# Second layer of a two-layer streaming encoder step: decays per batch, diagonal inverses, inner outputs in a shared bank

## Chip, core and metric

The kernel runs on one core of a Trainium2 chip. The metric is the time of one execution on the device, in microseconds (us). Before the change it is 1435.36 us, the median of three runs (1433.28 to 1436.85).

The engines are called PE (TensorE, matrix products), DVE (VectorE), ACT (ScalarE), POOL (GpSimd) and SP (SyncE, which here only issues transfers). Each works through its own queue in order. PE reads SBUF and writes PSUM; DVE and ACT read and write both; POOL is used on SBUF alone.

## The reference

The step has two layers over 1024 prompt frames and 64 sample frames of width 1024. The first has a gated convolution and band attention. The second, which the change touches, is a gated delta rule with 8 heads of width 128, in chunks of 64 frames (16 of the prompt, one of the sample, each group with its own start state):

```python
def gdn_chunk(S, q, k, v, g, beta):
    gc = jnp.cumsum(g, axis=1)
    decay = jnp.exp(jnp.where(incl, gct[..., :, None] - gct[..., None, :], -jnp.inf))
    kk = jnp.einsum('blhd,bmhd->bhlm', k, k)
    a = jnp.where(strict, bt[..., :, None] * kk * decay, 0.0)
    tmat = a + jnp.eye(L)
    rhs = concatenate([v * beta, k * (beta * exp(gc))])
    sol = triangular_solve(tmat, rhs, lower=True, unit_diagonal=True)
    u = sol[..., :HD_C] - einsum(sol[..., HD_C:], S)
    qk = einsum(q, k) * decay
    o = einsum(q * exp(gc), S) + einsum(qk, u)
    S_new = exp(g_last) * S + einsum(k * exp(g_last - gc), u)
```

Here `incl` is the lower triangle with its diagonal and `strict` the one without. Since `g` is negative, `gc` falls along a chunk, so the difference in `decay` is never positive where it is used.

## The kernel before

Activations lie with channels on the 128 partitions. A weight tile is 128 x 128 for each of eight k-tiles; every projection is made of three products (`hi` by `hi`, `hi` by `lo`, `lo` by `hi`) into a PSUM tile `pjt`, over three groups of 384, 384 and 320 frames. These `pjt<-...` products are most of PE's work in both layers.

The order of work on PE is written by the program itself: generators are registered with the class `Order`, and each `yield` names a time in ns after which the generator may go on, or the name of something that must be done. `Order.run` walks them by rank against a running estimate of PE's time. On the other engines the order comes from a scheduler of the tile framework, which also sets the waits.

In the second layer (`odd`) the heads are handled as four pairs, and the 17 chunks of a pair in three batches of 6, 6 and 5, so there are twelve batches. While `main` projects q, k and v of the next pair and, at the end, the gates z, each batch goes through these generators:

- `gates` (once): the cumulated decays `gc` and their exponentials, for all pairs.
- `decays` (once): for every pair and batch, the differences of `gc` between frames. DVE puts `gc` on a diagonal (L912), PE spreads it with a product of a block matrix (`tr<-dbuf,cst`), DVE subtracts (L916), POOL adds one of two masks with -1e30 outside a triangle (L919), ACT takes `Exp` (L920), and ACT's queue writes the strict and the transposed form to `Dd` in DRAM (L921).
- `prepare` (`prep`): loads the two decay tiles `Dst` and `DT`, transposes keys and queries on PE (`tr<-cst,kq`), takes squares on ACT (`junk`), makes key products (`tr<-kq`), and from them `An` and `KQD` (L984, L985). `Af`, the four diagonal 16 x 16 blocks of each head's matrix, is written to `Sd` in DRAM.
- `substitute` (`sub`): reads it back as `AL`, with one block in each of 48 partitions, does forward substitution in 14 steps of two POOL instructions (L1009, L1010), and writes the inverses to a second `Sd`.
- `join` (`inv`): loads the inverses as `Xf`, and POOL multiplies them with two masks into X, 32 wide with blocks on the diagonal (L1038). DVE transposes X into XT (L1039); PE products `tr<-XT,Cb`, `tr<-M,X` and `tr<-XT,An` put the larger inverse together.
- `solve` (`wy`): transposes and products that give the two right-hand sides.
- `scan`: chunk after chunk. PE makes `ks<-S,kq` (keys and queries on the state, two quarters of a PSUM bank), DVE `us` (L1158) and ACT `qs` (L1160) read it; PE makes `su<-us,kd`, and DVE two new states `S` (L1172). The inner outputs of the chunk before (`tr<-us,KQD`) are made in a `tr` bank just ahead of `ks`, and DVE adds `qs` to them (`o`, L1127).
- `finish`: normalizes four chunks of outputs and writes them to `od`.

The PSUM pool `pg` has two banks `tr`, which all of these share, two `su`, and one `ks`; the framework lets two engines read one PSUM tile only one behind the other (ACT's `qs` waits for DVE's `us`). A batch's `prep` waits for the `prep` before it, for `wy` two before and for `scan` three before; `sub` waits for the `sub` before it.

Of the kernel before, what the change touches and what calls it, by code (L numbers as in the profile page):

```python
# [7 lines left out]
F32 = mybir.dt.float32  # L8
# [31 lines left out]
C_M1, C_M2 = 448, 512  # L40
# [16 lines left out]
def constants():  # L57
# [10 lines left out]
    c[:, C_M1:C_M1 + 64] = np.where(j[None, :] < i[:, None], 0.0, NEG)  # L68
    c[:, C_M2:C_M2 + 64] = np.where(j[None, :] >= i[:, None], 0.0, NEG)
# [38 lines left out]
class Net:  # L108
# [124 lines left out]
    def run(self):  # L233
# [4 lines left out]
        with tc.tile_pool(name="pj", bufs=2, space=PSUM) as self.pj:  # L238
# [15 lines left out]
            self.Dd = [dram.tile([P, NCH, 64], F32, name=f"Dd{i}") for i in range(8)]  # L254
            self.Sd = [[dram.tile([m, P, 16], F32, name=f"Sd{a}{b}") for b, (c0, m) in enumerate(BATCHES)] for a in range(2)]
# [504 lines left out]
    def odd(self):  # L760
        nc, tc, I, O = self.nc, self.tc, self.I, self.O
        act, dve, pool, par, cst = self.act, self.dve, self.pool, self.par, self.cst
        w_in, mix, order, Dd, od, Sd = I["w_in1"], self.mixd[1], self.order, self.Dd, self.od, self.Sd
# [135 lines left out]
        def decays():  # L899
            gc = G["gc"]  # L900
            buf = G["buf"]

            def part(i, m):
                return buf[:, 384 * i:384 * i + 64 * m].rearrange("p (c j) -> p c j", j=64)

            for p in range(4):
                yield 0
                for c0, m in BATCHES:
                    sh = [P, m, 64]
                    gcb = gc[:, p, c0:c0 + m].unsqueeze(2).broadcast_to(sh)  # L910
                    gx, df = part(0, m), part(1, m)
                    dve.tensor_tensor(gx, gcb, cst[:, C_ID64:C_ID64 + 64].unsqueeze(1).broadcast_to(sh), ALU.mult)  # L912
# [3 lines left out]
                    dve.tensor_tensor(df, ps[:, :64 * m].rearrange("p (c j) -> p c j", j=64), gcb, ALU.subtract)  # L916
                    for q, (cm, op) in enumerate(((C_M1, ALU.subtract), (C_M2, ALU.add))):
                        dx = part(2 + q, m)
                        pool.tensor_tensor(dx, cst[:, cm:cm + 64].unsqueeze(1).broadcast_to(sh), df, op)  # L919
# [3 lines left out]
                order.done.add(f"dec{p}")  # L923
# [423 lines left out]
```

## Time and profile before

| what | value |
|---|---|
| median of the runs shown | 1435.36 us |
| profiled execution | 1453.08 us, its span 1451.3 us |
| mean granted PE clock of the profiled execution | 0.973 |
| busy share of the span: PE, DVE, ACT, POOL | 95%, 58%, 47%, 20% |
| second layer from the first decay to the last scan | about 690 to 1305 us |
| gates and output projection after it | to 1451 us |

The page gives busy time per engine and groups of instructions. A group names the line of the kernel (a helper's line for all products: L119 and L124), the engine, and output and input by tile names: `tr<-XT,Cb` is a product into a `tr` bank. Behind the bar stand the busy time, the mean of one instruction, and the idle time before it with its releaser. The views by windows give the same for stretches of time, with the granted clock of PE. Spans on POOL are rough.

### The profile page before, as it was taken

To read this page: it belongs to the slowest core of one execution; us is meant where nothing else is said; L and a number is where in the kernel's file an instruction comes from. 1 tells how busy PE (TensorE), PEld (TensorE's weight loads), DVE (VectorE), ACT (ScalarE), POOL (GpSimd) and SP (SyncE) were. 2 spreads that over 40 slices of the span, in tenths; PEclk is the share of its full clock that TensorE was granted. 3 is DMA by queue.
4 is the path that set the end of the run, shared out by engine and by line. 5 is a ranking of instruction groups with operands and counts; after the bars stand their busy time and mean duration, and the time that the engine had idled before them with its cause. 6 is when DMAs were issued, how large, how long until landed. Compare 5 with 4: busy or idle time off the path is not lost. (4 is left out here: it accounts for less than half of the span.)

```text
span 1451.3 us, 27914 instructions
## 1 busy us (share of the span) xinstructions
PE 1378.2 (95%) x10600; PEld 1238.7 (85%) x10600; DVE 839.1 (58%) x2220; ACT 676.9 (47%) x1776; POOL 289.8 (20%) x590
## 2 busy tenths in 40 slices
PE   8999999999999999899887999999999989999996
PEld 6989998998999899788776778778877877889995
DVE  7575257237436754786884668555765665433554
ACT  7643344144234456675554454435443534333752
POOL 3001000000100014420353325120423151300122
PEclk9999999999999999999998999999999999999998
DMA  8402111210210264540431112122321132336753
GB/s 270 132 23 82 57 52 52 79 53 27 89 61 30 81 234 141 188 145 31 115 96 52 29 40 71 27 42 49 71 34 42 37 100 59 98 104 205 244 199 117
DMA packets 113831, 132.71 MB, mean 91 GB/s; under 512 B 35280, under 2 KB 80792, under 8 KB 113696
## 3 DMA queue, kind: packets, MB, share of 16 engines
q1 hardware_dynamic: 82448, 104.32, 24.7%
q10 hardware_dynamic: 31248, 26.60, 5.7%
q8 instruction: 83, 1.36, 0.4%
q14 instruction: 52, 0.43, 0.1%
HBM read 99.71 MB, written 34.31 MB: 92 GB/s over the span
## 5 line engine op out<-in xcount | busy, mean ns | idle before, releaser
L119 PE MATMUL pjt<-hhi,wlo 128*128 128x384 f32 (+1 forms) x1768 | 618.7, 350 | 1.9 <-DVE wlo L165 1.9
L119 PE MATMUL pjt<-hhi,whi 128*128 128x384 f32 (+1 forms) x1768 | 584.8, 331 | 7.8 <-ACT whi L164 4.9
L119 PE MATMUL pjt<-hlo,whi 128*128 128x384 f32 (+1 forms) x1768 | 577.3, 330 | 1.1 <-DVE hlo L418 1.1
L119 PEld LDWEIGHTS pjt<-hhi,wlo 128*128 128x128 f32 x1768 | 338.0, 191 | 26.2 <-issue 12.4
L119 PEld LDWEIGHTS pjt<-hhi,whi 128*128 128x128 f32 x1768 | 338.5, 191 | 14.6 <-ACT whi L164 6.1
L119 PEld LDWEIGHTS pjt<-hlo,whi 128*128 128x128 f32 x1768 | 336.7, 191 | 2.0 <-DVE hlo L418 2.0
L165 DVE TENSOR_TENSOR wlo<-wf,whi 128x512 fp32r<-128x512 f32 x222 | 151.6, 707 | 165.8 <-ACT whi L164 162.1
L164 ACT CAST whi<-wf 128x512 fp32r<-128x512 f32 x222 | 130.4, 619 | 164.9 <-PE pjt L119 118.9
L639 ACT ACTIVATE pr<-pr,mx 128x640 f32<-128x640 f32 (+5 forms) x72 | 50.9, 707 | 89.4 <-DVE mx L638 88.9
L797 DVE SCALAR_TENSOR_TENSOR kq<-pjt,par,kq 128x384 f32<-128x384 f32 (+2 forms) x144 | 71.6, 497 | 3.4
L375 POOL TENSOR_TENSOR sqa<-sqa,sq 128x384 f32<-128x384 f32 (+1 forms) x36 | 39.3, 1091 | 142.0 <-ACT sq L372 141.9
L600 POOL MEMSET bias<- 64x64 f32 x8 | 1.5, 183 | 320.7 <-DMA bias<-Gd 295.6
L636 DVE CUSTOM_DVE_ANT_0 pr<-sc,bias 128x640 f32<-128x640 f32 (+5 forms) x72 | 47.9, 666 | 26.7 <-PE sc L119 25.9
L1172 DVE SCALAR_TENSOR_TENSOR S<-S,egl,su 128x128 f32<-128x128 f32 x128 | 40.2, 343 | 38.2 <-PE su L119 37.7
L1009 POOL TENSOR_TENSOR px<-AL 48x14 f32<-48x14 f32 (+6 forms) x168 | 46.5, 277 | 44.6 <-DMA AL<-Sd 33.2
L962 ACT ACTIVATE junk<-tr 128x128 f32<-128x128 f32 x136 | 37.7, 277 | 30.1 <-PE tr L124 24.5
L1010 POOL TENSOR_TENSOR AL<-AL,px 48x14 f32<-48x14 f32 (+6 forms) x168 | 48.1, 286 | 11.8
L1131 ACT ACTIVATE junk<-o 128x128 f32<-128x128 f32 x68 | 21.0, 309 | 57.4 <-DVE o L1127 52.4
L124 PE MATMUL pt<-cst,pr 128*128 128x128 f32 (+1 forms) x280 | 43.4, 270 | 4.4 <-DVE pr L641 2.9
L119 PE MATMUL ks<-S,kq 128*64 128x128 f32 x512 | 44.0, 295 | 0.0
L119 PE MATMUL pjt<-mhi,whi 128*128 128x384 f32 x128 | 43.0, 336 | 0.7 <-ACT whi L164 0.7
L119 PE MATMUL pjt<-mhi,wlo 128*128 128x384 f32 x128 | 43.0, 336 | 0.5 <-DVE wlo L165 0.5
(247 smaller groups left out, 2112.0 us busy)
## 6 DMA issues: line engine op xcount, KB each, us to landing
wf<-in_w_in SPq DMA_DIRECT2D x128, 256.0 KB, 3.1
wf<-in_w_out SPq DMA_DIRECT2D x96, 256.0 KB, 3.2
mf<-mixd SPq DMA_DIRECT2D x31, 192.0 KB, 4.2
x<-in_x SPq DMA_DIRECT2D x8, 384.0 KB, 5.5
xg<-in_x SPq DMA_DIRECT2D x2, 1536.0 KB
xd<-xg SPq DMA_DIRECT2D x2, 1536.0 KB
Dd<-dbuf ACTq DMA_DIRECT2D x16, 192.0 KB, 3.1
od<-o ACTq DMA_DIRECT2D x12, 256.0 KB, 2.2
```

The costliest lines, as they stand in the source:

```text
L119: return self.pe.matmul(out, lhsT=lhsT, rhs=rhs, start=start, stop=stop, **k)
L124: return self.pe.transpose(out, in_, self.ident[0:k, 0:k])
L164: self.act.copy(out=hi, in_=x)
L165: (eng or self.dve).tensor_tensor(lo, x, hi.bitcast(F32), ALU.subtract)
L375: pool.tensor_tensor(acc, acc, sq, ALU.add)
L636: dve.tensor_tensor_reduce(out=cut(pr[0:nq, :nk]), in0=sc[0:nq, :nk // nw, :nw], in1=cut(b["bias"][a][0:nq, j0:j0 + nk]), scale=1.0, scala ...
L639: act.activation(pr[0:nq, :nk], pr[0:nq, :nk], AF.Exp, bias=mx[0:nq, 1:2], scale=1.0, accum_out=mx[0:nq, 2:3])
L797: dve.scalar_tensor_tensor(oi, ch(ps[:, i0 + j + 1:i0 + j + 1 + m]), cw[j], oi, ALU.mult, ALU.add)
L962: act.activation(junk, ps[:, i, :], AF.Square, accum_out=ss[:, a, i0 + i:i0 + i + 1])
L1009: pool.tensor_tensor(t, AL[:, j + 1:16, j:j + 1].broadcast_to([lanes, m, w]), x.broadcast_to([lanes, m, w]), ALU.mult)
L1010: pool.tensor_tensor(o, o, t, ALU.add)
L1172: dve.scalar_tensor_tensor(Sn[:, q, :], S[:, q, :], egl[:, q, p, c:c + 1], su[q], ALU.mult, ALU.add)
```

## The change

It has three parts, all in the second layer.

Decays: the generator `decays`, its buffer and the DRAM tiles `Dd` go. Each batch makes its own decay in `prepare`, with a new generator `decay`: the diagonal of `gc` in the tile that becomes `An`, one product on PE, a subtraction by DVE inside the PSUM bank, then on ACT `Abs` and `Exp` with scale -1. So one symmetric tile `E` takes the place of two masked ones. The upper mask is a product on POOL (`KQD` = `E` times a matrix of ones and zeros), the strict lower one a product on DVE over `Af` (16 wide), one instruction more. `prep` waits for `gates` instead of its pair's decays.

Inverses: the second `Sd` is 32 wide, is filled with zeros once by three transfers on ACT's queue, and the inverses are written to its diagonal halves, even blocks left, odd blocks right. So X is loaded as it is, without `Xf` and the two POOL products. `AL` is loaded and the inverses are written in two transfers each, even and odd blocks. In `join` the second `yield` goes from 2250 to 1500.

Outputs: the inner outputs go to the third quarter of the `ks` bank of the next chunk. `outputs` is split: `inner` holds the products and stands where it stood, the DVE addition `o` comes after `us` and `qs`.

```diff
-            for p in range(4):
-                yield 0
-                for c0, m in BATCHES:
...
-                    gx, df = part(0, m), part(1, m)
-                    dve.tensor_tensor(gx, gcb, cst[:, C_ID64:C_ID64 + 64].unsqueeze(1).broadcast_to(sh), ALU.mult)
-                    yield 900
-                    ps = pst("tr")
-                    self.mm(ps[:, :64 * m], cst[:, C_BD:C_BD + P], gx.rearrange("p c j -> p (c j)"))
-                    dve.tensor_tensor(df, ps[:, :64 * m].rearrange("p (c j) -> p c j", j=64), gcb, ALU.subtract)
-                    for q, (cm, op) in enumerate(((C_M1, ALU.subtract), (C_M2, ALU.add))):
-                        dx = part(2 + q, m)
-                        pool.tensor_tensor(dx, cst[:, cm:cm + 64].unsqueeze(1).broadcast_to(sh), df, op)
-                        act.activation(dx, dx, AF.Exp)
-                        nc.scalar.dma_start(Dd[2 * p + q][:, c0:c0 + m, :], dx)
-                    yield 2500
+        def decay(e, gx, p, c0, m):
...
+            dve.tensor_tensor(gx, gcb, cst[:, C_ID64:C_ID64 + 64].unsqueeze(1).broadcast_to(sh), ALU.mult)
+            yield 900
+            ps = pst("tr")[:, :64 * m]
+            self.mm(ps, cst[:, C_BD:C_BD + P], gx.rearrange("p c j -> p (c j)"))
+            ps = ps.rearrange("p (c j) -> p c j", j=64)
+            dve.tensor_tensor(ps, ps, gcb, ALU.subtract)
+            act.activation(e, ps, AF.Abs)
+            act.activation(e, e, AF.Exp, scale=-1.0)
...
-            Dst, DT = bt("Dst", 64), bt("DT", 64)
-            nc.sync.dma_start(Dst, Dd[2 * p][:, c0:c0 + nb, :])
-            nc.sync.dma_start(DT, Dd[2 * p + 1][:, c0:c0 + nb, :])
+            E, An, KQD = bt("E", 64), bt("An", 64, 2), bt("KQD", 64, 3)
+            yield from decay(E, An, p, c0, nb)
...
+            pool.tensor_tensor(KQD, E, cst[:, C_UP:C_UP + 64].unsqueeze(1).broadcast_to([P, nb, 64]), ALU.mult)
...
+            dve.tensor_tensor(Af, Af, cst[:, C_LOW:C_LOW + 16].unsqueeze(1).broadcast_to([P, nb, 16]), ALU.mult)
...
-            nc.sync.dma_start(AL, sa.rearrange("c (b r) j -> (c b) r j", r=16))
+            even = sa.rearrange("c (b t r) j -> t (c b) r j", t=2, r=16)
+            diag = sx.rearrange("c (b t r) (s j) -> t s (c b) r j", t=2, r=16, s=2)
+            half = [slice(0, lanes // 2), slice(lanes // 2, lanes)]
+            for t in range(2):
+                nc.sync.dma_start(AL[half[t]], even[t])
...
-            nc.sync.dma_start(sx.rearrange("c (b r) j -> (c b) r j", r=16), AL)
+            for t in range(2):
+                nc.sync.dma_start(diag[t, t], AL[half[t]])
...
-            Xf = bt("Xf", 16)
-            nc.sync.dma_start(Xf, sx.rearrange("c r j -> r c j"))
+            X, XT = bt("X", 32), bt("XT", 32)
+            nc.sync.dma_start(X, sx.rearrange("c r j -> r c j"))
...
-            for j in range(2):
-                m = cst[:, C_H16 + j:C_H16 + j + 1].unsqueeze(2).broadcast_to([P, nb, 16])
-                pool.tensor_tensor(X[:, :, 16 * j:16 * j + 16], Xf, m, ALU.mult)
...
+                ks = pst("ks") if last or S is not None else None
                 if last:
-                    outputs(*last)
+                    inner(ks[:, 2 * P:3 * P], *last)
                 if S is not None:
-                    ks = pst("ks")
...
                     act.activation(qs, ks[:, P:2 * P], AF.Copy, scale=egc[:, p, c:c + 1])
+                if last:
+                    outputs(ks[:, 2 * P:3 * P], *last)
```

How the edit moves instructions shows at three places. The first is POOL in the substitution of the very first batch. `px` and `AL` are the steps, `dbuf` the decays' mask additions, `rk` and `kt` belong to the next batch's `prepare`. Before:

```order
L971 TENSOR_TENSOR rk<-rk,root 128x6
L1009 TENSOR_TENSOR px<-AL 48x36
L1010 TENSOR_TENSOR AL<-AL,px 48x12x3
L919 TENSOR_TENSOR dbuf<-cst,dbuf 128x384
L1009 TENSOR_TENSOR px<-AL 48x44
L919 TENSOR_TENSOR dbuf<-cst,dbuf 128x384
L975 TENSOR_TENSOR kt<-kt,kap 128x768
L1010 TENSOR_TENSOR AL<-AL,px 48x11x4
```

And after, at the later place where `rk` and `kt` stand now:

```order
L958 TENSOR_SCALAR rk<-ss 128x6
L1004 TENSOR_TENSOR AL<-AL,px 48x9x6
L959 TENSOR_TENSOR rk<-rk,root 128x6
L1003 TENSOR_TENSOR px<-AL 48x56
L1004 TENSOR_TENSOR AL<-AL,px 48x8x7
L1003 TENSOR_TENSOR px<-AL 48x56
L963 TENSOR_TENSOR kt<-kt,kap 128x768
L1004 TENSOR_TENSOR AL<-AL,px 48x7x8
```

The mask additions are gone from between the steps; the next batch's three instructions stay.

The second is DVE in a chunk of the second pair's scan, with the semaphores that a row waits for in brackets. Before:

```order
L1127 TENSOR_TENSOR o_8715<-tr,qs 128x128 [waits PE_49,Activation_49]
L1158 TENSOR_TENSOR us<-ks,vt 128x128 [waits PE_49]
L1172 SCALAR_TENSOR_TENSOR S<-S,egl,su 128x128 [waits PE_49] x2
L789 MEMSET pjt 128x3 [waits Activation_49]
L797 SCALAR_TENSOR_TENSOR kq<-pjt,par,kq 128x6x64 [waits DVE_49] x2
```

And after:

```order
L796 SCALAR_TENSOR_TENSOR kq<-pjt,par,kq 128x6x64 [waits DVE_49]
L1150 TENSOR_TENSOR us<-ks,vt 128x128 [waits PE_49]
L1119 TENSOR_TENSOR o_8570<-ks,qs 128x128 [waits Activation_49]
L1167 SCALAR_TENSOR_TENSOR S<-S,egl,su 128x128 [waits PE_49] x2
L1186 TENSOR_SCALAR o_8570<-o_8570,so 128x128 [waits Pool_49]
```

The addition `o` has moved behind `us`, waits for ACT (its `qs` reads the same bank), and stands ahead of the two new states.

The third is ACT at the `prepare` of the first pair's last batch. `junk` are the squares that free a `tr` bank, `kq<-kq` is a `Silu` of the projections, `E<-tr` the `Abs` and `E<-E` the `Exp` of the decay. Before:

```order
L962 ACTIVATE junk,ss<-tr 128x128 x2
L803 ACTIVATE kq<-kq 128x5x64
L962 ACTIVATE junk,ss<-tr 128x128 x2
L964 COPY kt<-tr 128x512
L784 ACTIVATE kq<-pjt,par 128x6x64
L1160 ACTIVATE qs<-ks,egc 128x128
```

And after:

```order
L950 ACTIVATE junk,ss<-tr 128x128
L908 ACTIVATE E<-tr 128x320
L950 ACTIVATE junk,ss<-tr 128x128
L909 ACT_TABLE_LOAD
L909 ACTIVATE E<-E 128x320
L950 ACTIVATE junk,ss<-tr 128x128
L1152 ACTIVATE qs<-ks,egc 128x128
L802 ACT_TABLE_LOAD
L802 ACTIVATE kq<-kq 128x5x64
```

The decay's two activations stand among the squares, with a load of the activation table ahead of `Exp` and another ahead of the next `Silu`.

More of the change, by code (lines that the diff above doesn't have):

```diff
@@ L39 @@
 C_ID64 = 384
-C_M1, C_M2 = 448, 512
+C_LOW, C_UP = 448, 512
 C_B16 = 576
@@ L253, in run @@
             self.Gd = [dram.tile([P, LROW], F32, name=f"Gd{h}") for h in range(8)]
-            self.Dd = [dram.tile([P, NCH, 64], F32, name=f"Dd{i}") for i in range(8)]
-            self.Sd = [[dram.tile([m, P, 16], F32, name=f"Sd{a}{b}") for b, (c0, m) in enumerate(BATCHES)] for a in range(2)]
+            self.Sd = [[dram.tile([m, P, 16 + 16 * a], F32, name=f"Sd{a}{b}") for b, (c0, m) in enumerate(BATCHES)] for a in range(2)]
             self.H = [None] * len(GROUPS)
@@ L762, in odd @@
         act, dve, pool, par, cst = self.act, self.dve, self.pool, self.par, self.cst
-        w_in, mix, order, Dd, od, Sd = I["w_in1"], self.mixd[1], self.order, self.Dd, self.od, self.Sd
+        w_in, mix, order, od, Sd = I["w_in1"], self.mixd[1], self.order, self.od, self.Sd
         NB = len(BATCHES)
@@ L931, in zeroed @@
                 pool.memset(Z[name], 0.0)
+            for b, (c0, m) in enumerate(BATCHES):
+                nc.scalar.dma_start(Sd[1][b].rearrange("c r j -> r c j"), Z["Cb"][:, :m, :])
             Z["root"] = self.kp.tile([P, 1], F32, name="root")
@@ L1117, in scan, with inner @@
             S = state.get(p)
-            def outputs(i, o4, so, u, qs):
-                o = pst("tr")[:, 0:P]
+            def inner(o, i, o4, so, u, qs):
                 for q in range(2):
@@ L1124, in outputs @@
                     self.mm(o[h], KQD[h, i, :], u[h], share=1.6, tile_position=(64 * q, 64 * q))
+            def outputs(o, i, o4, so, u, qs):
                 a = i % 4
@@ L1160, in scan @@
                     act.activation(qs, ks[:, P:2 * P], AF.Copy, scale=egc[:, p, c:c + 1])
+                if last:
+                    outputs(ks[:, 2 * P:3 * P], *last)
+                if S is not None:
                     yield 850
@@ L1177, in scan @@
                 yield 1110
-            outputs(*last)
+            ks = pst("ks")
+            inner(ks[:, 2 * P:3 * P], *last)
+            outputs(ks[:, 2 * P:3 * P], *last)
             if b == NB - 1:
@@ L1210, in add_pair @@
                 order.add(f"sub{n}", 1.6, substitute(p, b), [f"prep{n}"] + after("sub", n - 1))
-                order.add(f"prep{n}", 2, prepare(p, b), [f"dec{p}"] + after("prep", n - 1) + after("wy", n - 2) + after("scan", n - 3))
+                order.add(f"prep{n}", 2, prepare(p, b), ["gates"] + after("prep", n - 1) + after("wy", n - 2) + after("scan", n - 3))
         new_kq(0)
@@ L1232, in odd @@
                         order.add("gates", 2, gates(ba))
-                        order.add("decays", 3, decays(), ["gates"])
                     continue
@@ L1250, in odd @@
                     if p == 1:
-                        yield "decays"
+                        yield "gates"
                     new_v(p)
```

25 lines of the change are left out of this document (9 added, 16 removed).

## Prediction

> **What bounds the kernel now.** I read the page first, then the windows by stage, then the waits of TensorE (PE) in the stages that the edit touches.
>
> ```profile
> span 1451.3 us, 27914 instructions
> PE 1378.2 (95%) x10600; PEld 1238.7 (85%) x10600; DVE 839.1 (58%) x2220; ACT 676.9 (47%) x1776; POOL 289.8 (20%) x590
> 690.00:775.00 85.00, 66.37 (x436) 58.63 (x437) 65.99 (x164) 46.96 (x128) 39.28 (x66) 0.94 0.40 102
> 775.00:1300.00 525.00, 501.92 (x4955) 418.72 (x4947) 307.29 (x958) 226.09 (x767) 145.98 (x411) 0.96 0.23 55
> ```
>
> PE is the bound, and the edit neither adds nor removes a projection matmul. So it can win only where PE waits or runs at a lowered clock. The two rows of the windows are the second layer from the first decay to the end of the last scan: PE is idle for 85.00 - 66.37 = 18.6 us in the first stretch and 525.00 - 501.92 = 23.1 us in the second. (A windows row has its length and the busy us of PE, weight loads, DVE, ACT and POOL with their counts, then the granted clock, the DMA share and GB/s.) What ends those waits:
>
> ```profile
> PE tr L119 <- DVE XT L1039: 8.3, 1, 8.3
> PE tr L124 <- DVE dbuf L916: 3.9, 2, 2.6
> PE tr L119 <- ACT junk L962: 2.7, 2, 2.1
> PE tr L119 <- DVE dbuf L912: 2.2, 2, 1.2
> ...
> PE su L119 <- DVE us L1158: 7.8, 6, 3.1
> PE tr L119 <- DVE pjt L794: 4.4, 1, 4.4
> PE tr L124 <- DVE o L1127: 3.8, 3, 1.3
> ```
>
> The first four are of 690 to 775, the last three of 775 to 1300. The 4.4 us stand before the first `tr<-XT,Cb` product of the last pair, so they too are a wait for an inverse. Waits also cost clock. Windows cut at the changes of the granted clock (the value after the five counts) show it, and single projections on both sides of such a change:
>
> ```profile
> 719.80:723.20 3.40, 3.40 (x12) 3.40 (x13) 3.33 (x7) 2.57 (x11) 2.41 (x2) 0.50 0.68 206
> 767.60:781.30 13.70, 6.92 (x111) 5.98 (x111) 5.33 (x15) 3.45 (x6) 7.63 (x31) 0.50 0.14 40
> 808.60:815.40 6.80, 6.80 (x54) 5.19 (x54) 3.80 (x11) 3.04 (x14) 1.21 (x2) 0.50 0.01 2
> 1081.60:1091.90 10.30, 10.30 (x68) 7.59 (x68) 4.42 (x14) 4.46 (x16) 1.21 (x2) 0.50 0.01 2
> ...
> 683.66 0.47 PE L119 MATMUL pjt<-hhi,whi 128*128 128x320 f32 x1
> 683.93 0.47 PE L119 MATMUL pjt<-hlo,whi 128*128 128x320 f32 x1
> ...
> 686.04 0.31 PE L119 MATMUL pjt<-hlo,whi 128*128 128x320 f32 x1
> 686.19 0.31 PE L119 MATMUL pjt<-hhi,wlo 128*128 128x320 f32 x1
> ```
>
> At half clock two projections start 0.27 us apart, at full clock 0.15: 0.12 of every 0.27 us, 44%, is lost. The four windows hold 3.4, 6.9, 6.8 and 10.3 us of PE work, and cost 1.5, 3.0, 3.0 and 4.5 us.
>
> **The change, part by part.** The sum is made against the profiled execution, 1453.1 us (its span 1451.3 us and 1.8 around it), 1.2% over the median of 1435.4; I carry the difference over unchanged.
>
> *Decays made per batch.* Ten of the twelve decay products leave the stretch 690 to 775. There they fill both `tr` banks beside the transposes, and the waits on `dbuf` (3.9 and 2.2) and on `junk` (2.7, a bank held by the squares) are theirs: 8.8 us. Two products stay, and the built order puts both `An<-gc,cst` ahead of their need, so I leave 2 us: **-6.8**, and -1.5 for the window at 719.8. The ends are 0 and -10.3. The products themselves are only moved, and the ten later ones have their first operand ready long before PE comes.
>
> *First inverse.* The 8.3 us end with the substitution on POOL:
>
> ```profile
> 749.29 0.21 POOL L1009 TENSOR_TENSOR px<-AL 48x14 f32<-48x14 f32 x1 [2.71 <-DMA AL<-Sd]
> 753.40 1.01 POOL L919 TENSOR_TENSOR dbuf<-cst,dbuf 128x384 f32<-128x384 f32 x1
> 769.03 0.21 POOL L1010 TENSOR_TENSOR AL<-AL,px 48x14 f32<-48x14 f32 x1
> 773.26 0.65 POOL L1038 TENSOR_TENSOR X<-Xf,cst 128x96 f32<-128x96 f32 x2 [4.02 <-DMA Xf<-Sd]
> 773.98 0.21 POOL L1009 TENSOR_TENSOR px<-AL 48x14 f32<-48x14 f32 x1
> ...
> 783.11 0.21 POOL L1010 TENSOR_TENSOR AL<-AL,px 48x14 f32<-48x14 f32 x1
> ...
> 727.68 1.36 POOL L971 TENSOR_TENSOR rk<-rk,root 128x6 f32<-128x6 f32 x1
> 730.69 1.47 POOL L975 TENSOR_TENSOR kt<-kt,kap 128x768 f32<-128x768 f32 x1
> ```
>
> With decay additions between its steps it takes 749.3 to 769.2, 20 us; the next batch's, alone, takes 774.0 to 783.3, 9.3 us. After the change only `rk` and `kt` of the next batch stand between (1.4 + 1.5): some 12.4 us, 7.6 less, and 0.65 less for X, which is loaded ready-made. Against this, PE comes earlier: its waits of the part above are gone (6.8), and between the two points the order has four decay products fewer (0.88 us each in the row below) and some nine projections more (0.17 each), 2.0 us less. The transfers on SP stand closer:
>
> ```profile
> 710.40 0.88 PE L119 MATMUL tr<-dbuf,cst 128*128 128x384 f32 x2 [1.22 <-DVE dbuf L912]
> ...
> 741.19 0.37 SPq L993 DMA_DIRECT2D Sd<-Af  x1
> 741.79 0.94 SPq L158 DMA_DIRECT2D wf<-in_w_in  x2
> 747.38 0.33 SPq L1002 DMA_DIRECT2D AL<-Sd  x1
> ...
> Sd<-Af SPq DMA_DIRECT2D x8, 48.0 KB, 2.3
> AL<-Sd SPq DMA_DIRECT2D x8, 48.0 KB, 2.0
> Sd<-AL SPq DMA_DIRECT2D x8, 48.0 KB, 2.1
> ```
>
> Before, `AL` was issued 6.2 us after `Sd`, behind two weight loads; now it stands directly behind, some 2.3 us (one landing), 3.9 saved. The two split transfers each add an issue of 0.33. The chain shortens by 7.6 + 0.65 + 3.9 - 0.7 = 11.5, PE's arrival moves by up to 8.8: the wait falls by 2.7 if all of that comes, and is gone (8.3) if PE comes little earlier. I take 5.3, near the middle, leaving 3 us: **-5.3**, and -1.5 of the clock's 3.0. The ends are 0 and -11.3.
>
> *The other pairs' first inverses* wait 1.0 and 4.4 us in all today. For them the chain loses X on POOL (0.65), gains two issues (0.66), a mask on DVE, and a queued `KQD` on POOL ahead of the first step (about 1.0, as the decay addition above), while PE has, by the same count of rows, 0.2 to 2.3 us less to do. I take **+2**; ends -4 and +8. The write of the inverse now goes in 64-byte runs; the nearest row is `Sd<-Af`, which writes such runs, 2.3 against 2.1 us.
>
> *Inner outputs in the `ks` bank.* The three waits `tr <- o` (3.8 us) lose their reason; `us` is late in the same places, so I leave 1.3: **-2.5**. The windows at 808.6 and 1081.6 begin right behind two of them; I take half of their 7.5: -3.7. Ends 0 and -11.3. The new wait is on DVE: `o` reads a bank that ACT's `qs` also reads, and waits for it, with the two state updates `S` queued behind it, and PE's next `ks` behind those.
>
> ```profile
> 1287.44 0.29 DVE L1158 TENSOR_TENSOR us<-ks,vt 128x128 f32<-128x128 f32 x1 [0.30 <-PE ks L119]
> 1287.77 0.37 ACT L1160 ACTIVATE qs<-ks,egc 128x128 f32<-128x128 f32 x1
> 1289.09 0.60 DVE L1172 SCALAR_TENSOR_TENSOR S<-S,egl,su 128x128 f32<-128x128 f32 x2 [1.36 <-PE su L119]
> 1291.15 0.66 PE L119 MATMUL ks<-S,kq 128*64 128x128 f32 x8
> ```
>
> `qs` ends at 1288.14, `o` would end 0.3 later, and `S` does not start before 1289.09 anyway: 0.65 us of cover, and 1.46 us more from the end of `S` to the next `ks`. So `qs` may be 2.1 us later before PE feels it. I take nothing.
>
> *Activation tables.* `Exp` of the decays now stands among the `Silu` of the projections. The order has 21 table loads in this layer after the first gates where it had 5.
>
> ```profile
> 752.25 1.28 ACT L803 ACT_TABLE_LOAD   x1
> 753.55 0.53 ACT L803 ACTIVATE kq<-kq 128x384 f32<-128x384 f32 x1
> ```
>
> Sixteen more at 1.28 us are 20.5 us of ACT, which is busy 226 of 525 us. They fall among the copies and squares that free the `tr` banks, though the outputs' departure leaves each bank a turn longer. I take a quarter: **+5**, and +1.5 of clock. Ends 0 and +20.5. The Trainium skill, "ScalarE: Activation LUTs" (What ACT_TABLE_LOAD costs), counts a switch at about 2.66 us with a drain, and its rules say to group calls by table set, which this change undoes. The row above has the next `Silu` 1.30 us after the load's start, so no such drain shows here; by the page's figure ACT would have 42.6 us more, and the sum would be an estimated 5 us higher.
>
> *The rest:* DVE's transpose no longer waits for POOL's X, which holds `us` up in places: **-1** of the 7.8 (ends 0 and -5). POOL's other work and the removed `Dd` transfers hide under PE.
>
> Sum: -6.8 - 1.5 - 5.3 - 1.5 + 2 - 2.5 - 3.7 + 5 + 1.5 - 1 = -13.8, so 1439.3 for the profiled execution and **1421 us** for the median.
>
> The Trainium skill, "TensorE: Matmul & The Clock Gate" (Why this matters for your kernels), asks for no idle gap above about 3 us. The window of 1081.6 follows a wait of 1.3 us, so the row has drops after shorter ones; if the page held, the -3.7 would go and the sum would be some 1425 us.
>
> **The rivals.** *Slower: table loads in PE's way.* If every one of the sixteen reaches PE, at a `tr` bank or through `qs`, `o` and `S`, the +5 become +20.5, and ten 3.4 us windows of half clock (one for each pair of loads) add 10 x 3.4 x 0.44 = 15: 1435.4 - 20.3 + 20.5 + 15 = 1451; with half of both, 1433. It decides from about 1.3 us of PE per load. ACT's load of 43% and the 2.1 us of cover speak against it; that each falls into the transposes of its own batch speaks for it.
>
> *Only the prologue gains.* The wait for the inverses stays what it is, as PE arrives as much earlier as the chain is shorter, no clock window goes but the first, and tables cost 2: -8.3 + 2, 1429 us. The short distance between chain and PE order in first batches speaks for it; the plain 20 against 9.3 us against.
>
> *The gains cancel:* half of the table case, 1433 us, within 0.3% of before.
>
> **How the numbers follow.** About 0.3%, 4.3 us, is what a measurement of this kernel can tell from no change. Forecast (1403 to 1428) 0.57; prologue only 0.13; cancelled 0.16; slower 0.14. Faster: 0.57 + 0.13 = 0.70; same 0.16; slower 0.14. The range goes from 1403, where the ends of decays and clock are both met, to 1439, the middle of the way to the slower case.
>
> **What would show it.** Right: `PE <- dbuf` gone and the first 85 us short by 10 or more; the first substitution near 12 us; no `tr <- o`; fewer windows at 0.50. Wrong: PE waiting for `junk`, `vr` or `M` on ACT in the scans, `us` or `S` late behind `o`, or first inverses that hold PE more than 4 us in each pair.

## The result and the profile after

The changed kernel takes 1457.41 us (median of 4 runs, 1454.76 to 1462.66), the kernel before in the same comparison 1436.11: a ratio of 1.0124, with a 95% interval of 1.0078 to 1.017. It is slower by 1.2% where 1.0% faster was forecast. In the five later comparisons the kernel before has medians of 1448.2 to 1449.4 us, so from here on every time is a ratio to the kernel before, timed beside it.

The size of the loss is less certain than this interval. The changed kernel was timed in the first comparison alone, with four executions of each kernel, and nothing later repeats the 1436 us. Against the later medians its 1457.41 us would be 0.6% slower; the two profiled spans (1460.9 against 1451.3 us) differ by 0.7%. The first layer, which no edit touches, gives no sign of a faster chip: its last `pjt<-sq,mean` starts at 639.8 us in the changed kernel and at 638.0 to 641.2 in the other traces. The sign is the same by both ways of comparing, but each distance from the changed kernel to another below is about 0.9 points smaller by times than by ratios.

The profiled execution took 1462.66 us. From its page:

```profile
span 1460.9 us, 27782 instructions
PE 1390.1 (95%) x10600; PEld 1246.8 (85%) x10600; DVE 831.3 (57%) x2232; ACT 697.4 (48%) x1792; POOL 269.5 (18%) x554
```

PE has the same 10,600 products and is busy 11.9 us longer than before (1378.2). The windows by stage of the changed kernel, with the columns of the two rows of before:

```profile
690.00:775.00 85.00, 79.95 (x639) 73.58 (x637) 61.67 (x177) 42.45 (x129) 24.89 (x67) 0.96 0.23 45
775.00:1300.00 525.00, 491.82 (x4678) 404.40 (x4678) 301.08 (x950) 248.51 (x776) 140.97 (x373) 0.93 0.20 47
```

In the first 85 us PE is idle 5.1 us instead of 18.6: the prologue gives what was forecast. After it the granted clock falls from 0.96 to 0.93, and PE is idle 33.2 us instead of 23.1. (Both rows are fixed stretches of time; the changed kernel is further on in its work at 775.) PE's waits, first those of 690 to 776, then those of 775 to 1300 (what PE waited for, us in total, times, longest):

```profile
PE tr L119 <- DVE XT L1030: 2.2, 1, 2.2
...
PE tr L119 <- DVE kd L953: 6.1, 3, 2.9
...
PE su L119 <- DVE us L1150: 2.7, 3, 2.0
...
PE tr L119 <- DVE pjt L790: 2.4, 2, 1.4
PE tr L124 <- DVE kd L953: 2.1, 2, 1.4
```

The waits for `dbuf` are gone, the first inverse holds PE 2.2 us instead of 8.3, and `us` 2.7 instead of 7.8. Ahead of `tr` products PE now waits 8.2 us for `kd`: DVE reads a transpose of keys out of its `tr` bank (L953), and PE waits to use the bank again. In the kernel before that was, from 690 to 1300,

```profile
PE tr L119 <- DVE kd L965: 0.9, 1, 0.9
```

A windows table cut at the changes of the clock shows what follows two of these waits in the changed kernel:

```profile
777.40:794.50 17.10, 16.78 (x205) 12.96 (x205) 8.38 (x27) 6.33 (x25) 2.96 (x3) 0.50 0.00 1
...
907.20:910.60 3.40, 3.40 (x13) 2.93 (x12) 1.96 (x4) 1.88 (x5) 0.00 (x0) 0.50 0.00 0
917.40:934.50 17.10, 17.10 (x206) 12.98 (x194) 8.67 (x26) 7.29 (x24) 2.72 (x3) 0.50 0.01 2
```

Two stretches of 17.1 us run at half clock, each beginning within 0.3 us of the end of a wait for `kd`, with PE busy nearly all the time. At the 44% of the prediction they cost 14.9 us. Not every wait of this length has such a stretch behind it: in e4 below, waits of 2.9 us (to 700.1) and 3.0 us (to 1044.9) are followed by full clock. So that the wait brings on the stretch is read from where it begins; no run tests it by itself.

**An account of the profiled executions.** For each trace I added up two numbers from 600 us to PE's last product: PE's idle time, and PE's busy time inside stretches with a granted clock of 0.50. Idle plus 0.44 times the second is the loss. For the traces of the table its difference to that of the kernel before comes within 1.6 us of the difference of the profiled spans:

| kernel (profiled execution) | idle | at half clock | loss | less before's | span less before's |
|---|---|---|---|---|---|
| before | 50.9 | 58.8 | 76.8 | | |
| changed | 48.7 | 84.4 | 85.8 | +9.0 | +9.6 |
| e4, masked inverse | 47.1 | 28.2 | 59.5 | -17.3 | -16.8 |
| e5, changed with 2250 | 54.5 | 31.6 | 68.4 | -8.4 | -8.3 |
| e7, before plus table loads | 68.0 | 67.8 | 97.8 | +21.0 | +21.2 |
| e11, only the ks bank | 45.5 | 35.1 | 60.9 | -15.9 | -17.1 |
| e12, only the decays | 47.2 | 29.1 | 60.0 | -16.8 | -18.4 |
| e13, masked inverse, 1500 | 44.8 | 67.1 | 74.3 | -2.5 | -1.5 |
| e17, masked inverse, 3000 | 34.7 | 24.0 | 45.3 | -31.5 | -30.5 |

For the eleven traces not shown the two differences lie up to 4.5 us apart (e18, -29.5 against -25.0). The table is of one execution each, and that of the kernel before took 1453.08 us, 17.7 more than its median, so the table accounts for 9.6 us between the two kernels and not for the 21.3 between their medians.

The change takes 2.2 us off PE's waits and puts 25.6 us more of PE's work at half clock. So the question is what brings PE into those stretches.

### The profile page after: what moved, and what is told of

Same layout as the page of the kernel before. It is cut to its first block, busy times and chain, and to the rows that moved or that the text cites. A ratio compares the mean times of both kernels' runs of the same rounds, so it can differ in the third digit from the quotient of the medians.

```text
span 1460.9 us, 27782 instructions
## 1 busy us (share of the span) xinstructions
PE 1390.1 (95%) x10600; PEld 1246.8 (85%) x10600; DVE 831.3 (57%) x2232; ACT 697.4 (48%) x1792; POOL 269.5 (18%) x554
## 4 chain that ended last, share of the span: by engine, by line
PE 67%; DVE 9%; DMA 8%; ACT 7%; POOL 5%; issue 3%; SPq 1%; ACTq 0%; DVEq 0%; POOLq 0%
PE pjt L119 50%; PE tr L119 5%; PE ks L119 3%; DMA wf<-in_w_out 3%; PE sc L119 2%; PE pv L119 2%; PE pt L124 2%; PE tr L124 2%; PE su L119 1%; POOL sqb L330 1%; DVE wlo L165 1%; DMA X<-Sd 1%; POOL AL L1004 1%; ACT junk L950 1%; DVE pr L635 1%
## 5 line engine op out<-in xcount | busy, mean ns | idle before, releaser
L119 PEld LDWEIGHTS pjt<-hhi,wlo 128*128 128x128 f32 x1768 | 338.8, 192 | 27.5 <-issue 13.5
L638 ACT ACTIVATE pr<-pr,mx 128x640 f32<-128x640 f32 (+5 forms) x72 | 50.9, 707 | 89.4 <-DVE mx L637 88.8
L1003 POOL TENSOR_TENSOR px<-AL 48x14 f32<-48x14 f32 (+6 forms) x168 | 45.4, 270 | 57.1 <-DMA AL<-Sd 45.3
L1152 ACT ACTIVATE qs<-ks,egc 128x128 f32<-128x128 f32 x64 | 23.5, 367 | 62.2 <-DVE us L1150 62.1
L1004 POOL TENSOR_TENSOR AL<-AL,px 48x14 f32<-48x14 f32 (+6 forms) x168 | 50.0, 297 | 11.9
L1150 DVE TENSOR_TENSOR us<-ks,vt 128x128 f32<-128x128 f32 x64 | 18.5, 289 | 56.9 <-PE ks L119 56.4
L964 POOL TENSOR_TENSOR KQD<-E,cst 128x384 f32<-128x384 f32 (+1 forms) x12 | 11.6, 969 | 177.9 <-ACT E L909 177.9
```

The lines of the kernel that those rows point to most:

```text
L119: return self.pe.matmul(out, lhsT=lhsT, rhs=rhs, start=start, stop=stop, **k)
L638: act.activation(pr[0:nq, :nk], pr[0:nq, :nk], AF.Exp, bias=mx[0:nq, 1:2], scale=1.0, accum_out=mx[0:nq, 2:3])
L1003: pool.tensor_tensor(t, AL[:, j + 1:16, j:j + 1].broadcast_to([lanes, m, w]), x.broadcast_to([lanes, m, w]), ALU.mult)
L1004: pool.tensor_tensor(o, o, t, ALU.add)
```

## The experiments

The change has three parts, called D (decays per batch, with their table loads), X (inverses loaded wide, two transfers each way, and the second `yield` of `join` at 1500 in place of 2250) and K (inner outputs in the `ks` bank).

### One part undone at a time

**e1**, the changed kernel without the table switches:

```diff
-            act.activation(e, e, AF.Exp, scale=-1.0)
+            act.activation(e, e, AF.Silu, scale=-1.0)
```

> Changed kernel, with the Exp of each batch's decay replaced by Silu, so that the decay needs no other activation table than the projections beside it (the decays are then not the reference's; every instruction but the 20 table loads keeps its size). Theory, loads in PE's way: ACT is held for about 3 us at each of ten decays, the squares and copies that free the tr banks come late, PE waits and its clock drops; without the loads the time falls by 15 us or more from the changed kernel's 1457, to 1442 or less, and the half-clock windows between 690 and 1300 us fall below 65 us (now 81). Rival, the inner outputs in the ks bank: within 5 us of 1457. Rival, the inverses' longer chain (waits ahead of tr<-XT,Cb): within 5 us of 1457, and those waits stay. Rival, ten more decay products among the transposes: within 5 us of 1457.

Measured: 0.9837 (0.9797 to 0.9877), 1425.04 us; idle 35.4 us, 23.7 us at half clock. The half-clock windows between 690 and 1300 us come to 17 us, where the changed kernel has 75 (the 81 above counts two windows ahead of 690 as well). The loads are part of the loss. Since the data on PE are other ones here, e8 repeats the question with the decays of the reference.

**e2**, the changed kernel without K:

```diff
-                    inner(ks[:, 2 * P:3 * P], *last)
+                    outputs(*last)
...
+                o = pst("tr")[:, 0:P]
```

> Changed kernel, with the inner outputs and their additions back in the tr banks as before. Theory, table loads: the time stays within 6 us of the changed kernel's 1457. Rival, the ks bank (o behind qs, the states behind o, ks later): it falls by 10 us or more, to 1447 or less.

Measured: 1.0046 (1.0015 to 1.0077), 1454.02 us. By ratio it is back by 0.8%, between the two expectations; by time it is 3.4 us, within the 6 of the theory. PE's work at half clock falls from 84.4 to 60.8 us, while its idle time grows by 5.4. e11 and e10 show that K is no loss by itself; whether it is one in the changed kernel stays open.

**e3**, the kernel before with X and K, without D:

```diff
-                order.add(f"prep{n}", 2, prepare(p, b), ["gates"] + after("prep", n - 1) + after("wy", n - 2) + after("scan", n - 3))
+                order.add(f"prep{n}", 2, prepare(p, b), [f"dec{p}"] + after("prep", n - 1) + after("wy", n - 2) + after("scan", n - 3))
```

(and `decays`, `Dd`, `Dst` and `DT` as before.)

> Kernel before, with the diagonal inverses and the ks bank of the change, but the decays made ahead for all batches (masks on POOL, through DRAM) as before; 4 table loads between the first gates and the output gates as before. Theory, table loads: the time is that of before or below, 1440 or less. Rivals, the ks bank or the inverses: it stays at 1450 or more. The prediction's terms for these two parts (-2.5 and -3.7 for the bank, near nothing for the inverses) would give about 1430.

Measured: 1.0012 (0.9986 to 1.0038), 1450.26 us. Without any of the added table loads the gain of K (0.9909 in e11) is gone. So the loads are not the whole: X costs 1.0% on top of K.

**e4**, the changed kernel without X, that is D and K (from here "the masked kernel"):

```diff
-            for t in range(2):
-                nc.sync.dma_start(AL[half[t]], even[t])
+            nc.sync.dma_start(AL, sa.rearrange("c (b r) j -> (c b) r j", r=16))
...
+                pool.tensor_tensor(X[:, :, 16 * j:16 * j + 16], Xf, m, ALU.mult)
...
-            yield 1500
+            yield 2250
```

> Changed kernel, with the inverses loaded narrow and widened by two POOL products as before, one transfer each way. Theory, table loads: within 6 us of 1457. Rival, the inverses (two transfers each way, wider load): it falls by 8 us or more, and the slack between the transpose XT and the first tr<-XT,Cb grows in the first batches of a pair.

Measured: 0.9906 (0.9874 to 0.9938), 1436.24 us. My theory expected no change. With all its table loads this kernel is faster than before by 0.9%: the part that had looked like nothing carries the loss, as the rival said. The rival's sign did not come: in three of the four pairs' first batches `tr<-XT,Cb` still starts 0.15 us after the end of XT, as in the changed kernel.

### What in X costs: the order, the loads, the transfers

**e5**, the changed kernel with the old `yield` alone:

```diff
-            yield 1500
+            yield 2250
```

> Changed kernel, with the second yield of join at 2250 as before: no instruction is added or taken away, only PE's order around the first product of each inverse moves. The masked inverse with 2250 was 1436.2 beside 1448.7 of the kernel before, while the changed kernel was slower than before by 1.2%. Theory A, the order: with 2250 the time falls to at least 0.5% below the kernel before, timed beside it, as with the masked inverse. Theory B, the transfers (two each way, the wider load): it stays at 1.005 of before or more.

Measured: 0.9998 (0.9975 to 1.0021), 1448.09 us, between the two theories. One number in PE's order, with no instruction added or removed, is worth 1.26% by ratio (0.64% by time).

**e6**, the kernel before with the new `yield` alone:

```diff
-            yield 2250
+            yield 1500
```

> Kernel before, with the second yield of join at 1500 as in the change, nothing else: PE's order alone. Theory A, the order: slower than before by 0.5 to 1.5%, as PE comes to tr<-XT,Cb 0.75 us of its own work earlier, where it waited 13.7 us in all already. Theory B: within 0.4% of before.

Measured: 1.0059 (1.0035 to 1.0082), 1455.98 us. The early order costs 0.6% without the new table loads. But the wait that grows most is another one, for XT and not for a bank; from 690 to 1300:

```profile
PE tr L119 <- DVE XT L1039: 18.2, 3, 9.3
```

In the kernel before, 13.7 us stand ahead of `tr<-XT,Cb` products.

**e7**, the kernel before with table loads alone:

```diff
                     for i in range(m):
                         act.activation(junk, ps[:, i, :], AF.Square, accum_out=ss[:, a, i0 + i:i0 + i + 1])
+                        if i0 == a == 0 and i == 1:
+                            act.activation(dum, junk[:, 0:1], AF.Exp, scale=-1.0)
```

> Kernel before, with one Exp of a 128x1 tile added behind the second square of each batch: its result is not used, but it makes 20 more table loads (25 in this layer after the first gates, where the change has 21), at the place where the change has them. Theory, loads in PE's way: slower than before by 1.5 to 3% (the 2.9% between the changed kernel and the one without table switches), with more half-clock windows and waits for tr banks that ACT or DVE free late. Rival, the loads hurt only together with the rest of the change: within 0.7% of before. The prediction's term for the loads, 6.5 us, would be 0.45%.

Measured: 1.0122 (1.008 to 1.0164), 1466.76 us. The 20 loads cost 17.7 us (1.22% of 1449.42), 0.88 us each. That is less than the 1.5% expected, and more than twice the 0.41 us each of the prediction (6.5 for 16).

**e8**, the changed kernel without table switches and with its own decays:

```diff
-            half = ti % 8 < 2
+            half = True
```

(and the halved convolution weights kept for all heads.)

> Changed kernel, with the projections' Silu of all pairs in the form that the first heads have already (Tanh, which shares the table of Exp, and one DVE instruction more of about 0.6 us): the function is the reference's, 18 of the 20 later table loads are gone, some 48 DVE instructions (29 us of an engine that is busy 57%) are added. Theory, loads in PE's way: faster than before by 1% or more, near the 0.984 of the kernel with Silu in place of Exp. Rival, that gain came from the wrong decays or from DVE being free: within 0.5% of before or slower.

Measured: 0.9937 (0.9911 to 0.9962), 1439.42 us. So it is 1.9% better than the changed kernel by ratio (1.2% by time), although DVE has more to do. Against the kernel before it lies between the two expectations.

**e9**, both mended:

```diff
-            half = ti % 8 < 2
+            half = True
...
-            yield 1500
+            yield 2250
```

> Changed kernel with both losses mended: Tanh form of the projections' Silu (no table switches) and the second yield of join back at 2250. If the two add up: 0.9937 (Tanh alone) times 0.9875 (2250 alone, 0.9998 over 1.0124) is 0.981 of before. If they took away the same waits twice: between 0.988 and 0.994.

Measured: 0.9966 (0.9946 to 0.9987), 1444.65 us. The two don't add: this is even above the 0.988 to 0.994 that were expected if both took away the same waits. Four kernels that differ in these two things alone:

| whole change with | 1500 | 2250 |
|---|---|---|
| table loads | 1.0124 | 0.9998 (e5) |
| no table switches (Tanh) | 0.9937 (e8) | 0.9966 (e9) |

With the loads the early order costs 1.26% (0.64% by time); without them, in this kernel, it costs nothing that these intervals show.

**e10**, e9 without K (the edit of e2 on it):

```diff
-                    inner(ks[:, 2 * P:3 * P], *last)
+                    outputs(*last)
```

> The kernel with Tanh and 2250, and besides it the inner outputs back in the tr banks. The prediction's term for the ks bank, -6.2 us, would make this one 0.4% slower than the one with Tanh and 2250. Rival, the bank brings nothing or costs (the change with the inner outputs back was 1.0046 against 1.0124): equal or faster.

Measured: 1.0008 (0.9988 to 1.0028), 1451.66 us. The bank is worth 0.4% here, as predicted.

### The parts alone

**e11**, the kernel before with K alone:

```diff
-                    outputs(*last)
+                    inner(ks[:, 2 * P:3 * P], *last)
```

> Kernel before, with the inner outputs in the ks bank alone. The prediction's term, -6.2 us: 0.9957 of before, with no wait of a tr transpose for o. Rival, the bank brings nothing or costs: 1.000 or more, with waits ahead of ks<-us,KQD, ks<-S,kq or su<-us,kd that are longer than before's.

Measured: 0.9909 (0.988 to 0.9939), 1436.17 us, more than predicted. PE's waits of this kernel from 775 to 1300:

```profile
PE tr L119 <- DVE XT L1039: 15.3, 3, 8.2
PE su L119 <- DVE us L1159: 6.0, 8, 2.3
```

No `tr` product waits for the addition `o`, and no wait for `o` or `S` ahead of `ks` has taken its place. (The first row includes the first inverse's 8.2 us; in the kernel before, the same wait ends earlier and counts to the stretch up to 775.)

**e12**, the kernel before with D alone (the changed kernel with the edits of e2 and e4):

```diff
-            Dst, DT = bt("Dst", 64), bt("DT", 64)
+            E, An, KQD = bt("E", 64), bt("An", 64, 2), bt("KQD", 64, 3)
+            yield from decay(E, An, p, c0, nb)
```

> Kernel before, with the decays made per batch alone (16 more table loads, masked inverse, 2250, inner outputs in tr). The prediction's terms for this part, -6.8 -1.5 -5.3 -1.5 +2 +5 +1.5 = -6.6 us: 0.9954. With 17.5 us for the loads in place of 6.5 (1.22% for 20 of them on the kernel before): about 1.003. If the gain of the masked inverse (0.9906) came from the decays: 0.993 or less.

Measured: 0.9912 (0.9881 to 0.9943), 1435.65 us, again more than predicted, with all 16 more loads. D and K together (e4, 0.9906) bring no more than either; added up they would have been 0.982.

### The order and the transfers apart

**e13**, the masked kernel with the early order:

```diff
-            yield 2250
+            yield 1500
```

> Decays per batch and ks bank with the masked inverse (0.9906 of before with the second yield of join at 2250), and that yield at 1500. If the earlier order costs by itself beside the table loads: 1.000 to 1.005, as 2250 to 1500 cost 1.26% with the widened inverses. If it costs only together with the doubled transfers: within 0.3% of 0.9906.

Measured: 1.0005 (0.9982 to 1.0027), 1450.48 us. The order costs 1.0% without the doubled transfers too. This pair shows the mechanism best. The masked kernel (e4) first, PE between the transposes of keys and the second batch's first inverse product:

```profile
770.41 0.66 PE L124 MATMUL tr<-cst,kq 128*128 128x128 f32 x4
770.82 0.42 PE L119 MATMUL pjt<-hhi,wlo 128*128 128x384 f32 x1
...
772.41 0.66 PE L119 MATMUL ks<-S,kq 128*64 128x128 f32 x8
773.05 0.59 PE L119 MATMUL tr<-XT,Cb 32*32 32x16 f32 x48
```

Six projections, the inner outputs and the next `ks` stand between the two, and `tr<-XT,Cb` starts without a wait. The same place in e13, PE:

```profile
769.63 0.66 PE L124 MATMUL tr<-cst,kq 128*128 128x128 f32 x4
770.04 0.42 PE L119 MATMUL pjt<-hhi,wlo 128*128 128x384 f32 x1
770.30 0.34 PE L119 MATMUL pjt<-hhi,whi 128*128 128x384 f32 x1
770.47 0.34 PE L119 MATMUL pjt<-hlo,whi 128*128 128x384 f32 x1
773.72 0.65 PE L119 MATMUL tr<-XT,Cb 32*32 32x16 f32 x48 [2.90 <-DVE kd L951]
```

And e13's ACT there:

```profile
768.15 1.28 ACT L909 ACT_TABLE_LOAD   x1
769.44 0.47 ACT L909 ACTIVATE E<-E 128x320 f32<-128x320 f32 x1
...
770.44 1.28 ACT L802 ACT_TABLE_LOAD   x1
771.74 0.47 ACT L802 ACTIVATE kq<-kq 128x320 f32<-128x320 f32 x1
772.11 0.26 ACT L948 ACTIVATE junk<-tr 128x128 f32<-128x128 f32 x1
...
772.36 0.58 ACT L950 COPY kt<-tr 128x512 f32<-128x512 f32 x1
```

The load for `Exp`, the `Exp`, the load back and a `Silu` stand between the squares of one bank. The copy `kt` comes only at 772.36, and `kd` reads the same bank behind it. PE has three projections to do, then needs that bank. The edit has moved ACT too: in e4 only the first of the two loads stands ahead of `kt`.

```profile
771.68 0.59 ACT L950 COPY kt<-tr 128x512 f32<-128x512 f32 x1
...
775.04 1.28 ACT L802 ACT_TABLE_LOAD   x1
```

So the copy comes 1.3 us after the start of the transposes in e4 and 2.7 us after it in e13, and the two orders, PE's and ACT's, were not tried apart. What goes with the wait is in the clock, windows of e13 and then of e4 over the same two stretches:

```profile
774.10:791.20 17.10, 17.10 (x185) 12.75 (x174) 8.43 (x26) 6.18 (x22) 2.73 (x3) 0.50 0.00 1
907.20:924.30 17.10, 16.22 (x202) 12.40 (x203) 9.27 (x30) 7.55 (x28) 2.72 (x3) 0.50 0.01 3
```

```profile
774.10:791.20 17.10, 16.86 (x228) 13.05 (x227) 13.25 (x52) 9.76 (x31) 4.33 (x5) 1.00 0.01 2
907.20:924.30 17.10, 16.51 (x272) 12.47 (x270) 14.09 (x51) 10.81 (x40) 4.66 (x6) 1.00 0.01 2
```

The waits of these two kernels differ by 2 us in all, with less idle time in the slower one; the half-clock work differs by 38.9 us. The changed kernel has the same two stretches at 777.4 and 917.4; ahead of the second, only one load (913.03 to 914.31) stands between the squares, and PE waits 1.9 us.

**e14**, the masked kernel without table switches (the edit of e8):

```diff
-            half = ti % 8 < 2
+            half = True
```

> Decays per batch and ks bank with the masked inverse and 2250, and the Tanh form in place of Silu. If table loads cost wherever they stand: 0.980 or less, another 1% below 0.9906. If they cost only where PE comes early to the inverses (Tanh gained 0.3% beside 2250, 1.9% beside 1500): within 0.4% of 0.9906, since 48 more DVE instructions go against it.

Measured: 0.9925 (0.9899 to 0.9952), 1436.12 us, not distinct from e4. With the later order the loads cost nothing that can be seen, net of the 48 DVE instructions that come in their place.

**e15**, the masked kernel with two products moved off POOL:

```diff
-            pool.tensor_tensor(kt, kt, kap.unsqueeze(2).broadcast_to([P, nb, P]), ALU.mult)
-            pool.tensor_tensor(KQD, E, cst[:, C_UP:C_UP + 64].unsqueeze(1).broadcast_to([P, nb, 64]), ALU.mult)
+            dve.tensor_tensor(kt, kt, kap.unsqueeze(2).broadcast_to([P, nb, P]), ALU.mult)
+            dve.tensor_tensor(KQD, E, cst[:, C_UP:C_UP + 64].unsqueeze(1).broadcast_to([P, nb, 64]), ALU.mult)
```

> Decays per batch and ks bank with the masked inverse and 2250; the two products kt and KQD (1.5 and 0.9 us) go from POOL to DVE, so that in the first batch of a pair only rk stands between the steps of the substitution. If the first inverses are what is left: these substitutions fall from 13.5 to 15.8 us to about 11 to 13, the waits ahead of tr<-XT,Cb from 12.8 us by 5 or more, and the time to 0.986 or less. If DVE is then late elsewhere: 0.990 or more.

Measured: 0.9952 (0.993 to 0.9973), 1440.65 us. The expected gain did not come: the first substitutions took 12.0 to 14.5 us instead of 13.5 to 15.8, but the waits ahead of `tr<-XT,Cb` grew from 12.8 to 16.6 us.

**e16**, e5 with two buffers for the blocks:

```diff
-            AL = self.kp.tile([8 * NBM, 16, 16], F32, name="AL", tag="AL")[:lanes]
+            AL = self.kp.tile([8 * NBM, 16, 16], F32, name="AL", tag="AL", bufs=2)[:lanes]
```

> Changed kernel with 2250 (0.9998 of before) and two AL buffers, so that the load of the next batch's blocks doesn't wait for the two transfers that read the last one's. POOL waits 46.5 us for AL there, 17.5 with the masked inverse. If that buffer is what the doubled transfers cost: 0.993 to 0.996. If it is the transfers' own time and SP's queue: within 0.3% of 0.9998.

Measured: 0.9948 (0.9925 to 0.997), 1439.89 us. Of the 0.9% between e5 and e4, about half comes back. POOL's wait for the blocks in the masked kernel, in e5 and in e16:

```profile
POOL px L996 <- DMA AL<-Sd: 17.5, 9, 5.9
```

```profile
POOL px L1003 <- DMA AL<-Sd: 46.5, 11, 8.5
```

```profile
POOL px L1003 <- DMA AL<-Sd: 36.7, 11, 7.3
```

The buffer takes 9.8 of the 29.0 us that the widened inverses add. POOL's wait is no measure of the time, though: it is 33.2 us in the kernel before and 36.8 in e17 below, which has no doubled transfers and is the fastest with the reference's decays. Nearer to PE are its waits ahead of `tr<-XT,Cb`, 12.8 us in e4 and 17.2 in e5. The changed kernel shows one wait for the blocks; SP's queue (an issue and its us) and POOL's first step behind it:

```profile
743.58 0.38 SPq L982 DMA_DIRECT2D Sd<-Af  x1
744.05 0.95 SPq L1009 DMA_DIRECT2D Sd<-AL  x2
746.37 0.39 SPq L1021 DMA_DIRECT2D X<-Sd  x1
746.85 0.86 SPq L996 DMA_DIRECT2D AL<-Sd  x2
```

```profile
750.95 0.21 POOL L1003 TENSOR_TENSOR px<-AL 48x14 f32<-48x14 f32 x1 [7.32 <-DMA AL<-Sd]
```

The two writes of the old blocks, the load of X and the two loads of the new blocks follow each other, and the second batch's substitution starts 7.4 us after its `Af` was sent.

**e17**, the masked kernel with PE's order moved further the other way:

```diff
-            yield 2250
+            yield 3000
```

> Decays per batch, ks bank and masked inverse (0.9906 at 2250, 1.0005 at 1500), with the second yield of join at 3000. If PE still comes too early to the first product of an inverse: 0.985 or less, and the waits ahead of tr<-XT,Cb fall from 12.8 us. If the later inverses now hold up the scans: 0.990 or more.

Measured: 0.9864 (0.9824 to 0.9905), 1429.19 us, the fastest with the decays of the reference. From its page, and PE's waits from 690 to 1300:

```profile
span 1420.8 us, 27762 instructions
PE 1364.2 (96%) x10600; PEld 1227.6 (86%) x10600; DVE 829.7 (58%) x2232; ACT 695.6 (49%) x1792; POOL 277.7 (20%) x578
```

```profile
PE ks L119 <- DVE S L1165: 4.2, 1, 4.2
...
PE tr L119 <- DVE XT L1026: 3.2, 2, 1.8
```

The waits ahead of `tr<-XT,Cb`, 12.8 us in e4, are down to 3.5, and a wait for a state has appeared. The time lies between the two expectations. The step from 2250 is 0.4%, with intervals that overlap; from 1500 it is 1.4%.

**e18**, the whole change with two buffers and 3000:

```diff
-            AL = self.kp.tile([8 * NBM, 16, 16], F32, name="AL", tag="AL")[:lanes]
+            AL = self.kp.tile([8 * NBM, 16, 16], F32, name="AL", tag="AL", bufs=2)[:lanes]
...
-            yield 1500
+            yield 3000
```

> The whole change with two AL buffers (0.9948 at 2250), with 3000. Same two readings: 0.989 or less if PE still comes too early, 0.994 or more if the scans are held up.

Measured: 0.9887 (0.9847 to 0.9927), 1433.52 us. Two small edits turn the change from a loss into 1.1% faster than before.

## Why the prediction was wrong

**The step that failed** is the one that has no term. The working prices the loads and masks of the inverses, and gives the `yield` from 2250 to 1500 no price, though the part on the change names it; at most its count of rows ahead of the first inverses takes it in ("0.2 to 2.3 us less to do"). In the order that is 0.75 us of PE's own work by which `tr<-XT,Cb` comes earlier; e13 against e4 shows 1.0% for it, e5 against the changed kernel 1.26% by ratio and 0.64% by time. The prediction asked of the inverses only when they are ready. In the second batch of the changed kernel XT is ready at 765.3 us and used at 777.7. What is late there is the **bank**, in the same way as in e13: `tr<-XT,Cb` needs one of the two `tr` banks, which at this place hold the next batch's keys, and ACT with its two loads is behind:

```profile
764.92 0.38 DVE L1030 STREAM_TRANSPOSE XT<-X 128x192 f32<-128x192 f32 x1 [1.82 <-DMA X<-Sd]
...
772.15 1.28 ACT L909 ACT_TABLE_LOAD   x1
...
774.44 1.28 ACT L802 ACT_TABLE_LOAD   x1
...
776.36 0.58 ACT L952 COPY kt<-tr 128x512 f32<-128x512 f32 x1
...
776.97 0.69 DVE L953 TENSOR_TENSOR kd<-tr,dec 128x512 f32<-128x512 f32 x1 [1.71 <-ACT kt L952]
...
777.72 0.84 PE L119 MATMUL tr<-XT,Cb 32*32 32x16 f32 x48 [2.88 <-DVE kd L953]
```

(Start, us, engine and operation in the timeline of the changed kernel, with the idle time before it and what ended it.) The prediction's signs of being wrong name `junk`, `vr`, `M`, `us`, `S` and the first inverses; `kd`, and a second batch, are not among them.

**The tables** were mis-sized with it. "I take a quarter: +5, and +1.5 of clock" stands against 17.7 us for 20 loads in e7, and against 1.9% in the changed kernel (e8). The place was named rightly ("among the copies and squares that free the `tr` banks"), and so was the rival "table loads in PE's way", which had 1451 us for 1457.4. But a fixed share per load is the wrong form: beside 2250 and the masked inverse the loads cost nothing measurable (e14), beside 1500 they cost 1.9% by ratio and 1.2% by time (e8). Between these, what differs is whether PE has other work between the transposes and the next use of the bank. That is not the whole condition: in e7 the loads cost 1.2% beside 2250, in a kernel with the decays made ahead; why they do there was not followed.

**The clock** came out with the wrong sign. The prediction let windows go (-1.5, -1.5, -3.7) and added 1.5, with 3.4 us each in the slower rival. Two stretches last 17.1 us, and PE's work at half clock rose from 58.8 to 84.4 us, 11.3 us of time by the 44%. The Trainium skill, "TensorE: Matmul & The Clock Gate" (Part 1: The HAM clock gate), has full clock return after one busy window of about 3.4 us; here PE is busy 17.10 of 17.10 us at half clock, so the two differ, and the measurement decides.

**The transfers** of the widened inverses were counted as two issues more (0.66 us) against X on POOL (0.65). With the wider load in place of the masks they cost 0.9% (e5 against e4), about half of which a second AL buffer brings back (e16).

**Right in direction.** *Decay stalls:* gone; the first 85 us have 13.6 us less idle time, against 12.1 for this part and the first inverse together (-6.8 and -5.3). *First inverse:* 12.4 us of substitution were forecast; it takes from 730.2 to 743.6, 13.4 us,

```profile
730.23 0.21 POOL L1003 TENSOR_TENSOR px<-AL 48x14 f32<-48x14 f32 x1 [0.41 <-DMA AL<-Sd]
...
735.28 1.35 POOL L959 TENSOR_TENSOR rk<-rk,root 128x6 f32<-128x6 f32 x1
...
737.87 1.47 POOL L963 TENSOR_TENSOR kt<-kt,kap 128x768 f32<-128x768 f32 x1
...
743.34 0.28 POOL L1004 TENSOR_TENSOR AL<-AL,px 48x14 f32<-48x14 f32 x1
```

with `rk` and `kt` between the steps as the order had it, and PE waits 2.2 us for 3. *The ks bank:* no wait behind `o` took the place of the old one in e11, and K alone gives 0.9% for the 0.4% of the prediction. *D alone* gives 0.9% for 0.46%, loads included. Both terms were about half of what was measured.

**Wrong in sign, to the good:** *the other pairs' first inverses* fall from 5.4 to 2.4 us where +2 was taken (the row `tr <- DVE pjt L790` of 775 to 1300; XT ends 0.14 us ahead of both products, so it is XT that they wait for).

**The sum** took the terms as independent. D and K give 0.9% each and 0.9% together. Ahead of `tr<-XT,Cb` stand 13.7 us before, 8.5 with D alone (e12), 15.3 with K alone (e11) and 12.8 with both (e4), and 3000 takes most of that away; so part of what K saves beside D is met again as a wait for the next inverse. How the rest divides was not tried. A slip besides: the lower end of the range, 1403, does not come from "the ends of decays and clock" alone, which give about 1413; it takes the best ends of the first inverse and of the tables as well.

## What to carry over

Where an order is written by hand, a changed number in it is an edit with a price of its own: look up what stands before and behind the moved product, and which buffer it needs there, not only which operand. A short stall of an engine off the critical path (here two table loads of 1.28 us) costs little while the bound engine has other work before it needs the shared bank; where it had only three projections, PE waited 2.9 us. On a kernel like this, account for idle time and for work at half clock apart: the second moved the result here, with the first nearly unchanged.

## What was not expected of the hardware

After a wait of 1.9 to 2.9 us PE stayed at half clock for 17.1 us while it was busy 16.2 to 17.1 of them, in four stretches of two kernels (the changed one and e13); in the masked kernel the same windows had full clock at 16.5 to 16.9 us busy. All four hold an inverse's small products (`tr<-XT,Cb`, 32 x 32) between projections. They are not alone: e2 has a stretch of 17.1 us from 1070.7, all of it busy, after a wait of 1.6 us ahead of a transpose, and with other small products of an inverse (`tr<-M,X`, `tr<-XT,An`). The other stretches after 690 us last 3.4 to 13.7 us. What decides how long one lasts was not settled. (The profile models the ends of products, so idle moments between small ones may count as busy.)
